# Where the modulation dot products of a two-layer decoder trunk run, and how many steps lie between a unit's scores and its transposes

## The chip, the cores and the metric

The kernel runs on one core of a Trainium2 chip. The metric is the device time of one execution in microseconds (us), as the median of the runs shown. One execution was also taken with the hardware profiler. Its times are counted from its first instruction, and its span ends with its last.

TensorE (PE) multiplies matrices and transposes. VectorE (DVE) and ScalarE (ACT) do the elementwise work and empty PSUM, the memory that TensorE writes to. SyncE (SP) issues the loads of weights. POOL issues some others.

## The reference

Two layers run over 512 positions of width 1024. Each layer is

```python
mod = c_act @ w_ada + b_ada                      # six vectors of 1024: sh1 sc1 g1 sh2 sc2 g2
h = rmsnorm(x) * (1 + sc1) + sh1
u = h @ w_in                                     # pool, conv, q, k, v, three gates
merged = sum of sigmoid(gate_i) * (mixer_i(u) @ p_i)   # pooling, short convolution, attention
x = x + g1 * (merged @ w_out)
h2 = rmsnorm(x) * (1 + sc2) + sh2
x = x + g2 * ((silu(h2 @ w_gate) * (h2 @ w_up)) @ w_down)
```

The attention has 8 heads of 64, causal, in blocks of 256: a query sees its own block, and the past block where the gate allows it. The six vectors `mod` depend on `c` alone, so they may be computed at any time before their use: `g1` is first used after the output projection, `sc2` and `sh2` at the second norm.

## The kernel before

**Matmuls.** All large products are made three times with split operands (`mm3`, high times high, high times low, low times high, L149), so a weight tile of 128x1024 is loaded into a `raw` buffer (3 of them), split into `whi` by ACT (L325) and `wlo` by DVE (L328), and used by PE for eight triples. PE's instructions stand in program order. So do the instructions that the code pins on ACT and DVE, the splits and the dot products among them; the others are placed by a scheduler.

**Order of the work in a layer.** First comes the loop along k, eight steps that make q and three feature tiles; in layer 1 it begins with halves of three steps, and after the first of them `second` norms the rest. Three more feature tiles follow, then the k stage and the v stage (two calls of `wide`, four weight tiles each), two feature tiles for the convolution, 16 gate tiles with the pool and convolution products (`p1`, `p2` per step of eight, L909 to L929), and the list `GATE2`: eight more gate tiles, with the attention products put between. `drain()` stands before the first attention product and runs whatever attention work is left. The output projection and the feed-forward part follow.

**Ticks.** `mm3` counts columns. Every 2,048 columns, that is four triples of 512, it calls `tick()`. A tick first moves the attention on and then spends credit on queued small work.

**Attention as fibers.** `attention` is a generator that goes through four pairs of heads. For each it makes q and k features by transposes (`to_features`), then starts four units, one for each 128 queries. A unit makes its scores and the softmax (L594 to L619), then waits `WAIT[i]` ticks, transposes the probabilities (`tp`, L155) into PSUM tiles from which ACT and DVE copy them (L630, L631), waits two ticks, and multiplies with v (`po`). A unit with i of 2 or 3 needs two PSUM tiles for its transposes. A pair takes 12 ticks: q features at tick 3, k features at 4, units at 6, 8, 11 and 14, the next pair's q features at 15. At one tick the attention generator acts first, and then the units in the order of their start.

**PSUM.** The tag `mm` has four tiles. Gate tiles, `p1`, `p2`, features, transposes and `po` share them. Scores have a tag of their own, `pair`, with two tiles.

**Queued work.** `bulk` is a queue of small tasks with costs. Each tick adds `bulk_rate` to the credit, which is kept to at most 4.0, and tasks run while it is not negative. `flush_bulk()` runs all that is left. `ada_tasks` makes eight dot products for one of the six vectors, each with a cost of 1.2, and an end task of 0.2. A dot product (`ada_dot`, L374) is a DVE instruction over a tile of 128x1024 that SP has loaded. With `early` the tile is one of the three `raw` buffers that the weights use; without, one of the six `w4` buffers, of which four hold q and k from the end of the loop along k until the attention has used them.

Before the change, layer 0 runs `g1`, `sc2` and `sh2`, 24 dots, in `raw` buffers during the attention (rate 0.5). Layer 1 runs `g1` in the k and v stage in `w4` buffers, four dots before each of the two `wide` calls, and `sc2` and `sh2`, 16 dots, in the attention (rate 0.35).

Of the kernel before, what the change touches and what calls it, by code (L numbers as in the profile page):

```python
# [57 lines left out]
SH1, SC1, G1, SH2, SC2, G2 = range(6)  # L58
# [19 lines left out]
def hybrid_trunk(ctx, tc, xT, ws, ada, cols, pool_w, qk_w, crow, pos, con, out):  # L78
# [40 lines left out]
    bulk = deque()  # L119
    bulk_rate, credit = [0.0], [0.0]  # L120
# [36 lines left out]
    def mm3(o, lhs, rhs, start, stop, main=True, **more):  # L157
        matmul(o, lhs[0], rhs[0], start=start, stop=False, **more)
        matmul(o, lhs[0], rhs[1], start=False, stop=False, **more)
        matmul(o, lhs[1], rhs[0], start=False, stop=stop, **more)  # L160
        if main:
            clock[0] += o.shape[-1]
            if clock[0] >= TICK:
                clock[0] -= TICK
                tick()

    def cut(pair, *ix):
        return pair[0][ix], pair[1][ix]
# [163 lines left out]
    def load_w():  # L332
        while at[1] < min(at[0] + 1 + SUMS_AHEAD, len(items)):
            sums, sub = items[at[1]]
            if sums is not None and sub == 0:
                sums.begin()
            at[1] += 1
        sums, what = items[at[0]]
        at[0] += 1
        if sums is not None:  # L340
            return sums.load(what)
        l, blocks = what
        raw = rawt()
        fetch(raw, l, blocks)
        return split_w(raw, len(blocks))
# [3 lines left out]
    def next_w(ahead=None):  # L349
        ahead = ahead_now[0] if ahead is None else ahead  # L350
        while at[0] < len(items) and len(loaded) <= ahead:
            loaded.append(load_w())
        return loaded.popleft()

    def wblk(w, b):
        return w[0][:, b, :], w[1][:, b, :]

    def wrow(w, b0):
        return (w[0][:, b0:b0 + 4, :].rearrange("p b n -> p (b n)"),
                w[1][:, b0:b0 + 4, :].rearrange("p b n -> p (b n)"))  # L360
# [16 lines left out]
    def ada_first_load(j):  # L377
        tiles = {}
        for part in (SC1, SH1):
            tiles[part] = w4([P, D])  # L380
            nc.sync.dma_start(tiles[part], ada[0, part, j])
        return tiles
# [4 lines left out]
    def ada_first(j, tiles, part):  # L387
        pin(ada_dot(tiles[part], 0, part, j))
        m = mod[0][:, part, j:j + 1]
        if part == SC1:  # L390
            A.activation(amod[0][0][:, j:j + 1], m, AF.Identity, scale=colt[:, 0, C_N1 + j:C_N1 + j + 1],
                         bias=abias[:, j:j + 1])
        else:
            A.activation(m, m, AF.Identity, bias=colt[:, 0, C_ADA + part * KT + j:C_ADA + part * KT + j + 1])

    def ada_step(l, part, j, early):
        aw = wp.tile([P, D], F32, tag="raw", name=nm("raw"), bufs=RAW) if early else w4([P, D])
        nc.sync.dma_start(aw, ada[l, part, j])
        pin(ada_dot(aw, l, part, j))

    def ada_end(l, part):
        m = mod[l][:, part]
        V.tensor_add(m, m, colt[:, l, C_ADA + part * KT:C_ADA + (part + 1) * KT])
        if part in (SC1, SC2):
            fold_scale(l, 0 if part == SC1 else 1, 0, KT)
        if part == G1:
            V.tensor_scalar(m, m, 0.5, None, op0=ALU.mult)

    def ada_tasks(l, parts, early=False):
        out = []  # L410
        for part in parts:
            for j in range(KT):
                out.append((1.2, lambda part=part, j=j: ada_step(l, part, j, early)))
            out.append((0.2, lambda part=part: ada_end(l, part)))
        return out
# [101 lines left out]
    def second(nrm, l, i, bank):  # L517

        hold[0] = None
        nrm.stat(BLOCK, S, bank)  # L520
        for k, lo, hi in HALVES[3:] + REST:
            nrm.apply(l, i, k, lo, hi)
# [48 lines left out]


    GAP = (2, 3, 3, 3)
    WAIT = (2, 3, 3, 3)

    def unit(hp, i, q, k, v, y, nrq, prq):

# [40 lines left out]
        for a in range(2):  # L618
            V.tensor_scalar(pr[a][:, :w], pr[a][:, :w], den[:, a:a + 1], None, op0=ALU.mult)  # L619
        yield WAIT[i]  # L620

# [93 lines left out]
    for l in range(L):  # L715
# [7 lines left out]
        for n, (k, lo, hi) in enumerate([(k, 0, S) for k in range(KT)] if l == 0 else HALVES + REST):  # L723
            if l == 0:
                if k + 3 < KT:
                    first.append(ada_first_load(k + 3))
                if k + 2 < KT:
                    ada_first(k + 2, first[k + 2], SC1)
                    ada_first(k + 2, first[k + 2], SH1)
                    norm.first_scaled(k + 2)  # L730
                    norm.first_hi(k + 2)
                loaded.append(load_w())
                if k + 2 < KT:
                    norm.first_lo(k + 2)
            if k not in held:
                held[k] = next_w(0 if l == 0 else None)
            if l > 0 and n == 1:
                second(norm, l, 0, bank)
            w = held[k]
            h = norm.k(k)  # L740
            for t in range(lo // P, hi // P):
                mm3(q_ps[t], cut(h, slice(None), slice(t * P, (t + 1) * P)), wrow(w, 0), k == 0, k == KT - 1)
            for z in range(3):
                mm3(f_ps[z][:, lo:hi], wblk(w, 4 + z), cut(h, slice(None), slice(lo, hi)),
                    k == 0 and lo == 0, k == KT - 1)
# [100 lines left out]
            if j == 1:  # L846
                bulk.append((0, lambda: pool_chain(1, pool1)))

        gains = ada_tasks(l, (G1,)) if l > 0 else []
        bulk.extend(gains[:4])  # L850
        k_ps = wide()
        for t in range(TT):
# [45 lines left out]
        V.tensor_mul(cv[1], pb, cv[1])  # L898
        y_conv.append(split_from(cv[1]))

        bulk.extend(ada_tasks(l, (G1, SC2, SH2)[l:], True))
        bulk_rate[0] = (0.5, 0.35)[l]
        ahead_now[0] = 3

        def gate():
# [342 lines left out]
```

## Time and profile before

| what | value |
|---|---|
| median of 3 runs | 1481.39 us (1480.77 to 1481.45) |
| the profiled execution's own time | 1480.46 us |
| its span | 1478.7 us |
| PE, DVE, ACT busy | 1456.7, 1052.2, 666.3 us |
| mean granted TensorE clock | 0.999 |

The profiled execution is 0.93 us under the median, and 1.8 us of it lie around the span. A row of the groups or of the timeline gives a line of the code, an engine, what is written from what, and durations; a bracket at its end is the idle time of that engine just before and what ended it. A row of stretches gives the busy time of each engine between two times, the granted clock and the load of the DMA engines.

### The profile page before, as it was taken

The numbers are of one execution on the slowest core, as the hardware profiler recorded it, in microseconds if no ns is written. First come the engines' busy times: TensorE is split into PE (matmuls) and PEld (weight loads), VectorE is DVE, ScalarE is ACT, GpSimd is POOL, SyncE is SP. The second block draws the span as 40 slices with busy tenths as digits, with TensorE's granted clock in tenths as the row PEclk, the third lists the DMA queues.
The fourth block names the chain that finished last, engine by engine and source line by source line (L and its number), as shares of the span: only waits on it lengthen the run. The fifth ranks groups of instructions, "written<-read, shape, count | busy, mean of one in ns | idle before, by whom it ended". The sixth has DMA issues, their size and how long they took to land.

```text
span 1478.7 us, 21940 instructions
## 1 busy us (share of the span) xinstructions
PE 1456.7 (99%) x8443; PEld 1268.0 (86%) x8443; DVE 1052.2 (71%) x1855; ACT 666.3 (45%) x1138; POOL 105.8 (7%) x157
## 2 busy tenths in 40 slices
PE   8999999999999999999999999999999999999999
PEld 6888787778988998989988877778889889989997
DVE  7976887758686876767666777776586757657672
ACT  4634555443453352535444345455335525434350
POOL 0000000001100211210000000000010102111200
PEclk9999999999999999999999999999999999999999
DMA  9514433365337775744334443333462436637431
GB/s 346 199 73 159 141 136 134 115 227 148 109 114 221 207 190 174 198 113 117 114 109 146 155 143 126 102 114 128 143 193 81 141 114 167 191 89 196 131 105 65
DMA packets 84409, 217.19 MB, mean 147 GB/s; under 512 B 10832, under 2 KB 23760, under 8 KB 84304
## 3 DMA queue, kind: packets, MB, share of 16 engines
q1 hardware_dynamic: 67456, 177.37, 35.2%
q0 software_dynamic: 16128, 37.76, 11.6%
q8 instruction: 66, 1.08, 0.3%
q10 hardware_dynamic: 720, 0.66, 0.1%
q14 instruction: 39, 0.32, 0.1%
HBM read 213.65 MB, written 2.10 MB: 146 GB/s over the span
## 4 chain that ended last, share of the span: by engine, by line
PE 84%; DVE 8%; DMA 3%; ACT 3%; issue 1%; SPq 0%; DVEq 0%; ACTq 0%
PE mm L149 72%; PE pair L149 11%; DMA raw<-in_ws 2%; DVE wlo L328 2%; PE mm L155 1%; ACT whi L325 1%; DMA w<-in_ada 1%; DVE w L374 1%; DVE raw L374 1%; ACT tmp L612 0%; DMA x<-in_xT 0%; ACT tmp L614 0%; DVE big L914 0%; SPq L232 0%; DVE big L929 0%
## 5 line engine op out<-in xcount | busy, mean ns | idle before, releaser
L149 PE MATMUL mm<-big,whi 128*128 128x512 f32 (+1 forms) x4362 | 1083.3, 340 | 5.6 <-DVE tmp L1081 2.5
L149 PEld LDWEIGHTS mm<-big,whi 128*128 128x128 f32 x4362 | 746.0, 190 | 93.6 <-DVE tmp L1081 4.1
L149 PE MATMUL mm<-big,wlo 128*128 128x512 f32 (+1 forms) x2181 | 736.1, 337 | 0.0
L149 PEld LDWEIGHTS mm<-big,wlo 128*128 128x128 f32 x2181 | 413.9, 190 | 44.7
L325 ACT ACTIVATE whi<-raw 128x1024 fp32r<-128x1024 f32 (+2 forms) x240 | 248.8, 1039 | 298.3 <-PE mm L149 231.1
L328 DVE TENSOR_TENSOR wlo<-raw,whi 128x1024 fp32r<-128x1024 f32 (+2 forms) x240 | 284.7, 1193 | 81.9 <-ACT whi L325 81.0
L325 ACT ACTIVATE whi<-w 128x1024 fp32r<-128x1024 f32 x72 | 76.2, 1059 | 147.8 <-PE mm L149 107.7
L954 DVE SCALAR_TENSOR_TENSOR x<-mm,mod,x 128x512 f32<-128x512 f32 (+1 forms) x90 | 62.0, 689 | 101.4 <-PE mm L149 101.3
L254 POOL DMA_DIRECT2D w<-in_ws x72 | 48.5, 683 | 982.1 <-DVE w L374 377.3
L328 DVE TENSOR_TENSOR wlo<-w,whi 128x1024 fp32r<-128x1024 f32 x72 | 86.7, 1220 | 31.0 <-ACT whi L325 30.2
L149 PE MATMUL pair<-whi,big 128*128 128x512 f32 x224 | 76.7, 390 | 0.0
L256 POOL DMA_DIRECT2D w<-in_ws x72 | 64.6, 923 | 153.1 <-DMA w<-in_ws 136.3
L149 PE MATMUL pair<-big,whi 128*128 128x256 f32 (+1 forms) x376 | 74.0, 294 | 0.0
L374 DVE SCALAR_TENSOR_TENSOR w<-w,csil 128x1024 f32<-128x1024 f32 x56 | 66.9, 1220 | 9.5 <-DMA w<-in_ada 9.3
L149 PEld LDWEIGHTS pair<-big,whi 128*128 128x128 f32 x376 | 60.4, 191 | 2.2
L149 PE MATMUL mm<-whi,big 128*128 128x512 f32 x160 | 57.2, 394 | 1.7 <-ACT big L497 1.4
L149 PE MATMUL pair<-big,wlo 128*128 128x256 f32 (+1 forms) x188 | 55.3, 294 | 0.0
L511 DVE TENSOR_TENSOR big<-tmp,big 128x512 fp32r<-128x512 f32 x48 | 33.0, 690 | 24.3 <-ACT big L510 23.4
L149 PEld LDWEIGHTS pair<-whi,big 128*128 128x128 f32 x224 | 42.1, 188 | 8.7
L374 DVE SCALAR_TENSOR_TENSOR raw<-raw,csil 128x1024 f32<-128x1024 f32 x40 | 48.4, 1218 | 1.2 <-DMA raw<-in_ada 1.2
L914 DVE SCALAR_TENSOR_TENSOR big<-big,mm 128x512 f32<-128x512 f32 x48 | 32.6, 682 | 21.5 <-PE mm L149 21.1
L149 PE MATMUL pair<-wlo,big 128*128 128x512 f32 x112 | 43.6, 390 | 0.0
(187 smaller groups left out, 1251.5 us busy)
## 6 DMA issues: line engine op xcount, KB each, us to landing
raw<-in_ws SPq DMA_DIRECT2D x146, 512.0 KB, 3.4
w<-in_ws POOLq DMA_DIRECT2D x144, 256.0 KB, 4.6
w<-in_ada SPq DMA_DIRECT2D x56, 512.0 KB, 5.3
raw<-in_ada SPq DMA_DIRECT2D x40, 512.0 KB, 3.2
raw<-in_ws SPq DMA_DIRECT2D x64, 256.0 KB, 4.2
raw<-in_ws SPq DMA_DIRECT2D x24, 384.0 KB, 3.5
raw<-in_ws SPq DMA_DIRECT2D x16, 448.0 KB, 5.3
raw<-in_ws SPq DMA_DIRECT2D x36, 128.0 KB, 3.0
```

Source lines behind the costliest of these rows:

```text
L149: tc.keep_in_program_order(T.matmul(*a, **k))
L155: tc.keep_in_program_order(T.transpose(*a))
L254: nc.gpsimd.dma_start(dst, self.source(0, 1))
L256: nc.gpsimd.dma_start(dst, self.source(*other), accum_op=ALU.add)
L325: A.activation(hi[:, :n], raw[:, :n], AF.Copy)
L328: ins = V.tensor_sub(lo[:, :n], raw[:, :n], f32(hi)[:, :n])
L374: return V.scalar_tensor_tensor(aw, aw, 1.0, csil, op0=ALU.mult, op1=ALU.mult, accum_out=mod[l][:, part, j:j + 1])
L511: V.tensor_sub(lo, src, f32(hi))
L914: V.scalar_tensor_tensor(sg, sg, 1.0, branch, op0=ALU.add, op1=ALU.mult)
L954: V.scalar_tensor_tensor(x[k][:, lo:hi], src, mod[l][:, part, k:k + 1], x[k][:, lo:hi], op0=ALU.mult, op1=ALU.add)
```

## The change

`WAIT` goes from three to four ticks for units 2 and 3. The eight dots of `g1` of layer 0 go from the attention to the k and v stage, as in layer 1. The eight dots of `sc2` of layer 1 go from the attention into the loop along k, after `second`, in `w4` buffers. What is left in the attention is 16 dots in layer 0 (rate 0.35) and 8 in layer 1 (rate 0.18).

```diff
-    WAIT = (2, 3, 3, 3)
+    WAIT = (2, 3, 4, 4)
...
             if l > 0 and n == 1:
                 second(norm, l, 0, bank)
+                bulk.extend(ada_tasks(l, (SC2,)))
+                bulk_rate[0] = 0.6
...
-        gains = ada_tasks(l, (G1,)) if l > 0 else []
+        gains = ada_tasks(l, (G1,))
         bulk.extend(gains[:4])
...
-        bulk.extend(ada_tasks(l, (G1, SC2, SH2)[l:], True))
-        bulk_rate[0] = (0.5, 0.35)[l]
+        bulk.extend(ada_tasks(l, (SC2, SH2)[l:], True))
+        bulk_rate[0] = (0.35, 0.18)[l]
```

## Prediction

> **What bounds the kernel now.** I read the page first, then PE's waits, then stretches of the stages that the change touches, and last the timeline round the single waits.
>
> ```profile
> span 1478.7 us, 21940 instructions
> PE 1456.7 (99%) x8443; PEld 1268.0 (86%) x8443; DVE 1052.2 (71%) x1855; ACT 666.3 (45%) x1138; POOL 105.8 (7%) x157
> PE 84%; DVE 8%; DMA 3%; ACT 3%; issue 1%; SPq 0%; DVEq 0%; ACTq 0%
> ```
>
> PE is busy in all but 22.0 us of the span, and the change removes no matmul. So nothing can be won but waits of PE. These are the ones that matter here, in order of size (engine, line, what it waited for: us, times, longest):
>
> ```profile
> PE mm L155 <- DVE tmp L619: 4.7, 5, 1.9
> PE mm L149 <- DVE tmp L1081: 2.5, 8, 0.6
> PE mm L149 <- ACT big L909: 2.4, 1, 2.4
> PE mm L149 <- DVE big L914: 1.2, 1, 1.2
> PE mm L149 <- DVE big L890: 1.1, 1, 1.1
> PE mm L155 <- DVE big L514: 0.3, 1, 0.3
> ```
>
> The row with L1081 is the feed-forward part and stays. The others, 9.7 us, lie between the v stage and the output projection of the two layers. The stretches: k and v stage of layer 0 and of layer 1, attention of layer 0 and of layer 1, the second half of layer 1's loop along k, and 4 us after one wait.
>
> ```profile
> core 0: us, PE busy (x) PEld busy (x) DVE busy (x) ACT busy (x) POOL busy (x), PEclk, DMA share, GB/s
> 74.40:127.00 52.60, 52.60 (x235) 43.59 (x235) 37.56 (x91) 21.04 (x34) 0.00 (x0) 1.00 0.25 91
> 802.00:854.60 52.60, 51.48 (x229) 42.26 (x228) 43.22 (x92) 19.34 (x31) 0.00 (x0) 1.00 0.41 141
> 127.00:305.00 178.00, 173.95 (x907) 138.97 (x907) 140.91 (x333) 88.70 (x201) 0.00 (x0) 1.00 0.41 142
> 855.00:1034.00 179.00, 174.48 (x907) 140.11 (x905) 134.50 (x321) 89.79 (x203) 0.00 (x0) 0.99 0.37 126
> 763.00:784.00 21.00, 21.00 (x95) 17.38 (x94) 6.40 (x6) 6.17 (x8) 0.20 (x1) 1.00 0.37 126
> 943.00:945.00 2.00, 1.88 (x8) 1.79 (x9) 2.00 (x3) 0.78 (x3) 0.00 (x0) 0.50 0.00 0
> 945.00:947.00 2.00, 2.00 (x8) 1.58 (x7) 2.00 (x5) 0.24 (x1) 0.00 (x0) 0.69 0.44 162
> ```
>
> In the attention DVE is busy 79% (layer 0) and 75% (layer 1), and PE waits some 4 us in each. In the loop along k DVE is busy 30%. In layer 0's k and v stage it is busy 71% and PE never waits; in layer 1, with eight dots more, 82%, and PE waits once.
>
> **The dots.** One costs 1.22 us of DVE, in either buffer:
>
> ```profile
> L374 DVE SCALAR_TENSOR_TENSOR w<-w,csil 128x1024 f32<-128x1024 f32 x56 | 66.9, 1220 | 9.5 <-DMA w<-in_ada 9.3
> L374 DVE SCALAR_TENSOR_TENSOR raw<-raw,csil 128x1024 f32<-128x1024 f32 x40 | 48.4, 1218 | 1.2 <-DMA raw<-in_ada 1.2
> ```
>
> Eight are 9.8 us. Out of layer 0's attention, DVE falls there from 140.9 to 131.1 us (74%); out of layer 1's, from 134.5 to 124.7 us (70%). None of this is PE's time; what it is worth is the waits that it feeds.
>
> *One wait behind a late weight.* In layer 1:
>
> ```profile
> 921.78 0.33 SPq L398 DMA_DIRECT2D raw<-in_ada  x1
> 924.55 10.15 SPq L232 DMA_DIRECT2D raw<-in_ws  x2
> 933.08 1.23 DVE L328 TENSOR_TENSOR wlo<-raw,whi 128x1024 fp32r<-128x1024 f32 x1
> 938.75 1.06 ACT L325 ACTIVATE whi<-raw 128x1024 fp32r<-128x1024 f32 x1 [3.77 <-DMA raw<-in_ws]
> 943.12 1.65 PE L149 MATMUL mm<-w,big 128*128 128x256 f32 x6 [2.36 <-ACT big L909]
> 943.89 1.22 DVE L374 SCALAR_TENSOR_TENSOR raw<-raw,csil 128x1024 f32<-128x1024 f32 x1
> ```
>
> A dot's tile was loaded at 921.78 and used at 943.89: one of three `raw` buffers was held for 22 us. The second weight load of 924.55 had to wait until the split at 933.08 freed another, ACT stood 3.77 us for it, the exponentials and the gate's tanh (L909) queued behind, and PE's `po` stood 2.36 us for the PSUM tile that the tanh frees. Then the granted clock was 0.50 for 2 us and 0.69 for 2 us, 1.6 us of work. So this event costs 2.4 + 1.6 = 4.0 us. The Trainium skill ("TensorE: Matmul & The Clock Gate", Why this matters for your kernels) says that the clock falls back for idle gaps above about 3 us; by it the event would have cost 2.4 us and the sum below would be 1.6 us smaller. The trace shows the fall after 2.36 us, and I go by the trace. With half as many dots in layer 1 a dot's tile stands in the way half as often: **-4.0**. Layer 0 gets the number of dots and the rate that layer 1 had, so such an event may come there: between 0 and 4.0, taken at a quarter since 16 dots made one in one layer and 24 none in the other: **+1.0**.
>
> *Backlog of DVE in layer 0.* The waits for L914 and L514 (1.2 + 0.3 us), both for PSUM tiles that DVE empties late, go with 9.8 us less work: **-1.5**, between -1.5 and 0.
>
> *The k and v stage of layer 0.* It gets what layer 1 has. There the multiplication that frees the tile for the last convolution product came late:
>
> ```profile
> 123.39 0.69 DVE L890 TENSOR_TENSOR big<-mm,big 128x512 f32<-128x512 f32 x1 [0.85 <-PE mm L149]
> 853.29 0.68 DVE L890 TENSOR_TENSOR big<-mm,big 128x512 f32<-128x512 f32 x1
> 854.12 0.70 PE L149 MATMUL mm<-big,whi 128*128 128x512 f32 x2 [1.11 <-DVE big L890]
> ```
>
> In layer 0 DVE stood idle for PE before it, in layer 1 it was behind, and PE waited 1.11 us. Layer 0 would come to 37.56 + 9.8 = 47.3 us of 52.6, 4 us above layer 1's 43.2 (the rotary tables' work among it). So 1.11 us, up to 1.1 + 4 if all of the difference came late; most of it lies ahead of idle time, so **+1.6**, between 0 and 5.
>
> *The loop along k of layer 1.* DVE has 14.6 us idle in the 21 us shown, in gaps such as this one:
>
> ```profile
> 772.40 1.22 DVE L328 TENSOR_TENSOR wlo<-raw,whi 128x1024 fp32r<-128x1024 f32 x1 [3.53 <-ACT whi L325]
> ...
> w<-in_ada SPq DMA_DIRECT2D x56, 512.0 KB, 5.3
> ```
>
> The queue is empty when the dots come, so the saved credit of 4.0 issues four at the first tick and one every other tick after. A burst of 4.9 us delays the norms of the later k-steps by as much. On SP the seventh load waits for the first dot's `w4` buffer, and weights queue behind, but they are fetched three tiles ahead. The eight loads of 512 KB, 4.2 MB, fit beside a DMA share of 0.37. I take **0**, between 0 and 1.1 (the L890 row, if one norm comes late). If that cover were gone, all eight dots, 9.8 us, would be PE's.
>
> **The fourth step.** A tick is four triples, 12 matmuls, and 12 take:
>
> ```profile
> 36.93 2.72 PE mm L149 x12
> ```
>
> So transposes of units 2 and 3 come at least 2.7 us later. The longest of the five waits for L619 (the normalised probabilities) is 1.9 us, so all should end: **-4.7**, between -4.7 and 0. Two things come in their place.
>
> First, unit 2's transposes move from unit 3's start to the tick of the next pair's q features. Then q features and two transposes, three of the four `mm` tiles, are taken at once beside the running gate. Three places per layer (the last pair has no next), six in all. The same place now:
>
> ```profile
> 162.15 0.87 PE L155 MATMUL mm<-ident,tmp 128*128 128x128 f32 x6
> 165.30 0.55 DVE L631 TENSOR_TENSOR w<-mm,w 128x384 fp32r<-128x384 f32 x1
> 165.60 0.60 PE L155 MATMUL mm<-ident,w 128*128 128x128 f32 x4
> 165.83 1.22 DVE L374 SCALAR_TENSOR_TENSOR raw<-raw,csil 128x1024 f32<-128x1024 f32 x1
> 167.05 0.68 DVE L914 SCALAR_TENSOR_TENSOR big<-big,mm 128x512 f32<-128x512 f32 x1
> ```
>
> The q features start at 165.60, so the third tile would be wanted near 166.4, and the product `p2` left its tile only at 167.73: 1.3 us late. But a dot (1.22 us) and the copy of unit 2's transposes stood ahead of it on DVE, and the copy moves behind. A place costs between 0 and 2.4 us (the L909 row); I take 0.25, nearest to the places that do not wait at all: **+1.5** for six.
>
> Second, the last unit's `po` comes one tick nearer to the attention product that needs it:
>
> ```profile
> 310.34 1.11 PE L149 MATMUL mm<-w,big 128*128 128x256 f32 x8
> 315.39 0.29 DVE L649 TENSOR_TENSOR big<-tmp,big 128x128 fp32r<-128x128 f32 x1 [0.38 <-ACT big L648]
> 318.32 0.69 DVE L914 SCALAR_TENSOR_TENSOR big<-big,mm 128x512 f32<-128x512 f32 x1 [2.64 <-PE mm L149]
> ```
>
> From the end of `po` (311.3) to that of L649 (315.7) are 4.4 us. The first attention product ended near 318.2, and its last triple, which needs the result, began 0.7 us earlier, at 317.5: 1.8 us to spare, less 2.7 us is 0.9 us short in layer 0. Part of the 4.4 us was ACT behind a late weight, so **+0.4**, between 0 and 0.9.
>
> **The sum**: -4.0 + 1.0 - 1.5 + 1.6 + 0 - 4.7 + 1.5 + 0.4 = -5.7 us. From 1480.46, the profiled execution's own time, that is 1474.8; the median of the runs is 0.93 us above that execution, so 1475.7. With every gain and no cost it is -10.2 us, 1471.2.
>
> **Rivals.**
> *The waits move and the gain is given back.* DVE is still busy 70 to 74% in the attention, the first tick there still issues four dots at once from saved credit, and a PE that no longer waits reaches the next late tile sooner. If half of the 10.2 us returns and layer 0's k and v stage and the PSUM places cost 1.6 + 1.5 + 0.4, it is -1.6 us: 1479.8. For it: waits on L914, L514 and L909 exist already. Against: the loads leave the stages where they are. That the dots do not run where they are queued comes out here too, since credit only decides the tick.
>
> *PSUM tiles (slower).* The three transposes-worth of tiles at one tick do wait, at all six places. Without that term the sum is -7.2 us, so from 1.2 us a place the change loses; at 2.0 us, between the L914 and the L909 rows, it is +4.8 us: 1486.2. For it: the 1.3 us above. Against: with that copy and some dots gone, DVE empties `p2` earlier. The Trainium skill ("Perfetto Trace Analysis", Optimization Strategy) says that a gap repeating on the engine that should be saturated can mean too few PSUM tiles; no row here shows six such gaps.
>
> *DVE over its measure in layer 0's k and v stage.* At 47.3 of 52.6 us a late rotary table or pool step pushes the chain that ends in L890. At the bound of +5 the sum is -2.3 us, 1479.1; it needs late attention on top to lose.
>
> **How the numbers follow.** Forecast 0.60, waits given back or the k and v stage at its bound 0.22, PSUM tiles 0.16, still more gain 0.02. A measurement of this kernel can tell about 0.2%, 3.0 us, from no change. Forecast and more gain are faster (0.62), the second group is within it (0.21, with a little of it beyond), the third slower (0.17). The forecast's own range is 1471.2 to 1478.4; with the others, leaving out the worst of the PSUM case, 1471 to 1485.
>
> **What would show it.** Right: no PE wait for L619; none for L909 in layer 1's attention, and the clock at 1.00 there; a wait for L890 of 1 to 2 us in both layers; PE without waits in layer 1's loop along k. Wrong: waits of L155 or L149 at q features for L914, L631 or L909; a PE wait before the first attention product over 0.9 us; a wait for L328 or L484 in layer 1's loop.

## The result and the profile after

The kernel got slower: 1487.17 us (1486.28 to 1487.35, five runs) against 1480.77 us (1477.67 to 1481.45, five runs) for the kernel before. The ratio is 1.0048, interval 1.0034 to 1.0063. The forecast was 1475.7 us with a range from 1471 to 1485, so the sign was wrong. The time is near that of the rival "PSUM tiles (slower)", 1486.2 us, which had a chance of 0.16; how far that is luck is said below.

Lines of the helpers keep their numbers up to L738. The tanh of a gate tile was L909 and is L911, the products behind it were L914 and are L916, L890 is L892, and L1081 is L1083.

The head of the page after, with the busy times:

```profile
span 1485.4 us, 21924 instructions
PE 1462.2 (98%) x8443; PEld 1273.5 (86%) x8443; DVE 1057.4 (71%) x1855; ACT 664.8 (45%) x1138; POOL 105.8 (7%) x157
```

The span grew by 6.7 us. PE's busy time grew by 5.5 us of that, with the same 8443 matmuls, so most of the growth is not idle time: 4.7 us of it is work that ran at a lower clock (the ledger below has 6.3 us of that after, and the prediction 1.6 us before). Its idle time went from 22.0 to 23.2 us. PE's waits after:

```profile
PE mm L149 <- ACT big L911: 8.6, 3, 4.0
PE mm L155 <- DVE big L514: 2.8, 1, 2.8
...
PE mm L149 <- DVE big L892: 1.0, 1, 1.0
```

The five waits for L619 and the one for L914 are gone. The tanh, with one wait of 2.4 us before, has 8.6 us in three, and L514 has one of 2.8 us. The stretches that the forecast named, in the same order (k and v stage of layer 0, attention of layer 0, second half of layer 1's loop along k), and then 4 us behind the wait for L514 and 6 to 7 us behind each of the two long waits for L911:

```profile
core 0: us, PE busy (x) PEld busy (x) DVE busy (x) ACT busy (x) POOL busy (x), PEclk, DMA share, GB/s
74.40:127.00 52.60, 52.45 (x233) 42.96 (x232) 44.62 (x106) 19.45 (x32) 0.00 (x0) 1.00 0.43 141
127.00:305.00 178.00, 175.19 (x906) 140.99 (x905) 137.30 (x320) 89.97 (x204) 0.00 (x0) 0.99 0.36 123
763.00:784.00 21.00, 21.00 (x94) 17.42 (x93) 15.56 (x24) 7.01 (x10) 0.31 (x1) 1.00 0.55 184
215.00:217.00 2.00, 2.00 (x9) 1.61 (x8) 1.46 (x4) 0.69 (x1) 0.00 (x0) 0.59 0.88 264
217.00:219.00 2.00, 2.00 (x7) 1.56 (x6) 1.09 (x1) 0.98 (x2) 0.00 (x0) 0.56 0.20 80
940.00:941.00 1.00, 0.97 (x2) 0.83 (x3) 1.00 (x4) 0.00 (x0) 0.00 (x0) 0.50 0.00 0
941.00:943.00 2.00, 2.00 (x6) 1.57 (x5) 1.19 (x2) 0.00 (x0) 0.00 (x0) 0.50 0.00 0
943.00:945.00 2.00, 2.00 (x6) 1.52 (x6) 0.00 (x0) 0.00 (x0) 0.00 (x0) 0.50 0.74 262
945.00:947.00 2.00, 2.00 (x11) 1.64 (x10) 0.08 (x1) 0.69 (x1) 0.00 (x0) 0.80 0.00 0
989.00:991.00 2.00, 1.97 (x7) 1.60 (x8) 2.00 (x4) 0.00 (x0) 0.00 (x0) 0.80 0.00 0
991.00:993.00 2.00, 2.00 (x7) 1.51 (x6) 0.79 (x2) 0.00 (x0) 0.00 (x0) 0.50 0.35 115
993.00:995.00 2.00, 2.00 (x11) 1.62 (x10) 1.29 (x2) 0.69 (x1) 0.00 (x0) 0.85 0.41 156
```

The dots in layer 1's loop along k cost nothing: seven of the eight lie in this stretch, DVE went from 6.40 to 15.56 us and PE stayed at 21.00 of 21. With eight more in layer 0's k and v stage, DVE went from 37.56 to 44.62 us and PE from 52.60 to 52.45. In layer 0's attention the dots fell from 28.01 to 19.48 us, but DVE's busy time in the stretch stayed where it was, 140.99 us after 140.91: other work filled it. The last eight rows show a clock of 0.50 to 0.85 behind each long wait.

**Where the waits stand.** At the tick of a next pair's q features, four transposes for these and six of unit 2 now run in one row. The timeline of PE at the three places that waited long:

```profile
207.95 0.60 PE L155 MATMUL mm<-ident,w 128*128 128x128 f32 x4
208.38 0.82 PE L155 MATMUL mm<-ident,tmp 128*128 128x128 f32 x6
...
214.79 0.66 PE L155 MATMUL mm<-ident,w 128*128 128x128 f32 x4 [2.81 <-DVE big L514]
...
934.80 0.60 PE L155 MATMUL mm<-ident,w 128*128 128x128 f32 x4
935.24 0.82 PE L155 MATMUL mm<-ident,tmp 128*128 128x128 f32 x6
940.03 1.22 PE L149 MATMUL mm<-big,whi 128*128 128x512 f32 x2 [3.97 <-ACT big L911]
...
983.94 0.60 PE L155 MATMUL mm<-ident,w 128*128 128x128 f32 x4
984.38 0.82 PE L155 MATMUL mm<-ident,tmp 128*128 128x128 f32 x6
989.03 0.72 PE L149 MATMUL mm<-big,whi 128*128 128x512 f32 x2 [3.83 <-ACT big L911]
```

At both places in layer 1 the row of ten transposes stands right behind the last triple of a gate tile. They take three of the four `mm` tiles, the finished gate product holds the fourth, and the next gate tile can't begin until the tanh has emptied it. What ACT does meanwhile at the second place:

```profile
934.77 1.06 ACT L325 ACTIVATE whi<-raw 128x1024 fp32r<-128x1024 f32 x1 [2.34 <-PE mm L149]
935.86 0.56 ACT L612 ACTIVATE tmp<-pair,asm,nrq 128x256 f32<-128x256 f32 x1
...
937.50 0.56 ACT L614 ACTIVATE tmp<-pair,asm,nrq 128x256 f32<-128x256 f32 x1
...
938.04 0.69 ACT L513 ACTIVATE big<-mm,colt 128x512 fp32r<-128x512 f32 x1
938.61 0.88 ACT L630 ACTIVATE w<-mm 128x384 fp32r<-128x384 f32 x2
939.35 0.63 ACT L911 ACTIVATE big<-mm 128x512 f32<-128x512 f32 x1
```

The gate's last product is complete near 935.0. The tanh starts at 939.35, behind a weight's split, four exponentials of a unit's softmax, the q features' copy and the two copies of unit 2's transposes. ACT is busy all the time; PE stands still for 3.97 us.

In layer 0 the ticks fall two triples into a gate tile, so PE has gate work left at this point, and the next to want a tile are the k features. There DVE was behind:

```profile
211.71 1.22 DVE L374 SCALAR_TENSOR_TENSOR raw<-raw,csil 128x1024 f32<-128x1024 f32 x1
...
212.85 1.22 DVE L328 TENSOR_TENSOR wlo<-raw,whi 128x1024 fp32r<-128x1024 f32 x1
213.99 0.75 DVE L514 SCALAR_TENSOR_TENSOR big<-mm,colt,big 128x512 fp32r<-128x512 f32 x1
```

A dot and a split, 2.4 us, stand ahead of the L514 that frees the q features' tile.

**The ledger.** With what the clock lost behind them (two microseconds at 0.59 lose 2 x 0.41), the three events cost 2.81 + 1.7, 3.97 + 2.9 and 3.83 + 1.7 us, 16.9 in all; a third wait for L911 is 0.8 us. Gone are 4.7 us for L619, 2.4 + 1.6 for the old event at L909, 1.2 for L914 and 0.3 for the old L514, 10.2 in all. 17.7 less 10.2 is 7.5 us, against 6.7 us of span. PE's waits elsewhere in the kernel are 1.8 us shorter after than before, so about 1 us of the growth is in none of these items.

### The profile page after: what moved, and what is told of

It is laid out like the page before. It is cut to its first block, busy times and chain, and to the rows that moved or that the text cites. A ratio compares the mean times of both kernels' runs of the same rounds, so it can differ in the third digit from the quotient of the medians.

```text
span 1485.4 us, 21924 instructions
## 1 busy us (share of the span) xinstructions
PE 1462.2 (98%) x8443; PEld 1273.5 (86%) x8443; DVE 1057.4 (71%) x1855; ACT 664.8 (45%) x1138; POOL 105.8 (7%) x157
## 4 chain that ended last, share of the span: by engine, by line
PE 87%; DVE 6%; ACT 3%; DMA 3%; issue 1%; SPq 0%; DVEq 0%; ACTq 0%
PE mm L149 75%; PE pair L149 11%; DMA raw<-in_ws 2%; DVE wlo L328 2%; PE mm L155 1%; ACT whi L325 1%; DMA w<-in_ada 1%; DVE w L374 0%; DVE raw L374 0%; DMA x<-in_xT 0%; SPq L232 0%; ACT tmp L614 0%; ACT tmp L612 0%; DVE tmp L1083 0%; DVE tmp L481 0%
## 5 line engine op out<-in xcount | busy, mean ns | idle before, releaser
L374 DVE SCALAR_TENSOR_TENSOR w<-w,csil 128x1024 f32<-128x1024 f32 x72 | 86.3, 1224 | 10.1 <-DMA w<-in_ada 9.9
L916 DVE SCALAR_TENSOR_TENSOR big<-big,mm 128x512 f32<-128x512 f32 x48 | 32.7, 686 | 25.9 <-PE mm L149 25.5
L510 ACT ACTIVATE big<-tmp 128x512 fp32r<-128x512 f32 x48 | 29.5, 620 | 20.7 <-DVE tmp L808 11.0
```

What stands on the lines that cost most here:

```text
L374: return V.scalar_tensor_tensor(aw, aw, 1.0, csil, op0=ALU.mult, op1=ALU.mult, accum_out=mod[l][:, part, j:j + 1])
L510: A.activation(hi, src, AF.Copy)
L916: V.scalar_tensor_tensor(sg, sg, 1.0, branch, op0=ALU.add, op1=ALU.mult)
```

## The experiments

The theory: the loss is the fourth step's alone, by the tiles that unit 2's transposes take at the tick of the next q features, with evacuations queued behind other work. One rival is that the moved dots cost more than they bring; another that the step is bad by what it does to unit 3 or to `po`. Ratios are to the kernel before, run beside it on the same chip, in five rounds each. The experiments ran on three chips, and the kernel before does not take the same time on each, so from chip to chip only ratios are compared.

**The dots alone.** The kernel after, with

```diff
-    WAIT = (2, 3, 4, 4)
+    WAIT = (2, 3, 3, 3)
```

> The dots are moved as in the change, the fourth step is left out (WAIT 2, 3, 3, 3). PSUM theory (the changed kernel loses some 17 us at three of the six places where unit 2's transposes and the next pair's q features take three of the four mm tiles at one tick): the ten transposes in a row are gone and with them these waits; some of the waits for L619 return, at most 4.7 us; 1471 to 1477 us. Rival, the dots (the loads and DVE work put into the k and v stage and the loop along k push attention work late): the time stays at 1483 us or more.

Measured: 1471.66 us against 1482.95, ratio 0.9928 (0.9913 to 0.9943). PE's waits of this kernel that lie in the changed stages:

```profile
PE mm L149 <- ACT big L911: 0.5, 1, 0.5
...
PE mm L155 <- DVE tmp L619: 0.3, 1, 0.3
```

The moved dots bring about 0.7%. The wait for L619 is down to 0.3 us, in a kernel whose fourth step is undone: moving the dots cured the five waits of before. In the profiled executions the time fell by 1480.46 - 1471.5 = 9.0 us and PE's idle time by 8.5 us, from 22.0 to 13.5. Most of that are the waits named here: 4.4 at L619, 2.4 - 0.5 at the tanh, 1.0 + 0.3 at L914 (now L916, 0.2 left) and L514, 0.2 at L892 (0.9 left), less a new 0.5 at L616, in sum 7.3. The 1.6 us of clock behind the old event at L909 are gone too, but this execution lost 1.7 us of clock behind a wait of 1.80 us near its start.

**The fourth step alone.** The kernel before, with

```diff
-    WAIT = (2, 3, 3, 3)
+    WAIT = (2, 3, 4, 4)
```

> The kernel before with the fourth step alone (WAIT 2, 3, 4, 4), all dots where they were. PSUM theory: the waits for L619 go (5 us), the waits at the six places come, with more dots in the way of the copies than in the changed kernel; 1483 to 1492 us. Rival, the dots: the step alone only gains, 1474 to 1478 us.

Measured: 1484.64 us against 1482.95, ratio 1.0013 (1.0002 to 1.0024). PE's waits of this kernel:

```profile
PE mm L149 <- ACT big L909: 4.6, 2, 3.8
PE mm L149 <- DVE big L914: 2.5, 2, 1.6
...
PE mm L149 <- DVE big L514: 1.9, 1, 1.9
...
PE mm L155 <- DVE big L514: 1.7, 1, 1.7
```

The waits for L619 are traded for waits on PSUM tiles, with little net. On top of the moved dots the same step costs far more, 1.0048 against 0.9928. By the spans it is 15.7 us there and 5.4 us here. Of the 10.3 us between them, 4.4 are that it has almost no wait for L619 left to remove, and 3.3 that the clock fell behind more of the new waits; the rest is in the waits themselves.

**Which unit's step.** The kernel after, with `WAIT` of unit 3 alone raised,

```diff
-    WAIT = (2, 3, 4, 4)
+    WAIT = (2, 3, 3, 4)
```

> The changed kernel with the fourth step for unit 3 alone (WAIT 2, 3, 3, 4), so that unit 2's transposes keep their tick with unit 3's scores and no tick takes three mm tiles. PSUM theory: the waits at the six places go, those for L619 come back for unit 2 only, 1 to 2 us; 1469 to 1475 us. Rival, the dots: 1483 us or more.

and with that of unit 2 alone:

```diff
-    WAIT = (2, 3, 4, 4)
+    WAIT = (2, 3, 4, 3)
```

> The changed kernel with the fourth step for unit 2 alone (WAIT 2, 3, 4, 3). PSUM theory: the ten transposes in a row and the waits behind them are all there; 1483 to 1489 us. Rival (it takes both steps together to fill the tiles): 1471 to 1476 us.

Measured: 1471.14 us, ratio 0.9922 (0.9907 to 0.9937), for unit 3, and 1488.18 us, ratio 1.0064 (1.005 to 1.0078), for unit 2. PE's waits with unit 2's step alone:

```profile
PE mm L149 <- ACT big L911: 8.6, 4, 4.0
PE mm L155 <- DVE big L514: 4.5, 2, 2.8
```

Unit 2's step is the whole loss. Unit 3's can't be told from nothing: 0.9922 against 0.9928 without it. With unit 3's alone no wait for L619 came back, where 1 to 2 us were expected; two short ones for L911, 1.4 us in sum, are left.

**Room elsewhere for unit 2's transposes.** If the `mm` tiles are what is short, transposes that take another place should not wait. In the first try they went to the two halves of a tile with the tag of the scores:

```diff
+        two = ps_pair() if i == 2 else None
...
-            tp = ps_mm().rearrange("p (j a q) -> p j a q", a=n, q=P)[:, :i + 1]
+            room = ps_mm() if two is None else two[:, aa[0]]
+            tp = room.rearrange("p (j a q) -> p j a q", a=n, q=P)[:, :i + 1]
```

> The changed kernel, but unit 2's transposes go into one pair tile (two banks) in place of two mm tiles; the step and the dots stay. PSUM theory: the ten transposes still run in a row, PE no longer waits for L911 or L514 behind them, the waits for L619 stay away; 1468 to 1473 us. Rival, the order on ACT (the gate's tanh stands behind eight exponentials and three copies, whatever tiles there are): PE still waits at these places, 1480 us or more. Rival, the dots: 1483 us or more.

Measured: 1522.45 us, ratio 1.0265 (1.0247 to 1.0282). PE's waits of this kernel:

```profile
PE pair L155 <- DVE w L633: 36.0, 8, 6.4
...
PE mm L149 <- ACT big L913: 0.8, 1, 0.8
```

This missed for a reason of its own. The loop copies the first set before it writes the second; in two tiles these overlap, but in one tile the second set waited for the copies of the first, eight times, 36.0 us. The wait for the tanh did fall, from 8.6 to 0.8 us. The second try writes both sets first and then copies both:

```diff
+        tps = []
+        for aa in groups:
+            room = ps_mm() if two is None else two[:, aa[0]]
...
+            tps.append(tp)
+        for aa, tp in zip(groups, tps):
```

> The changed kernel with unit 2's transposes in one pair tile, as in the run before that, but both sets of transposes are issued before the first copy, so that the second set does not wait for the copies of the first (that wait was 36.0 us in eight places). PSUM theory: neither that wait nor those behind ten transposes in a row (13 to 17 us in the changed kernel) are left; 1468 to 1474 us. Rival, the order on ACT (the tanh late behind exponentials and copies, whatever tiles there are): PE still waits for L911, 1480 us or more.

Measured: 1472.5 us against 1478.94, ratio 0.9955 (0.9942 to 0.9967). The place in layer 1, from the timelines of PE and ACT (the tanh is L916 here, the copy L635):

```profile
931.79 0.60 PE L155 MATMUL mm<-ident,w 128*128 128x128 f32 x4
932.22 0.82 PE L155 MATMUL pair<-ident,tmp 128*128 128x128 f32 x6
...
932.84 0.56 ACT L612 ACTIVATE tmp<-pair,asm,nrq 128x256 f32<-128x256 f32 x1
...
935.03 0.70 ACT L513 ACTIVATE big<-mm,colt 128x512 fp32r<-128x512 f32 x1
935.60 0.50 ACT L635 ACTIVATE w<-pair 128x384 fp32r<-128x384 f32 x1
935.97 0.62 ACT L916 ACTIVATE big<-mm 128x512 f32<-128x512 f32 x1
```

The same ten transposes stand in a row and the tanh is about as late behind the same exponentials, but two `mm` tiles are free and PE has no long wait here. So neither the ten transposes nor ACT's load does it alone: the tiles must be short as well. One new wait came, 1.64 us in layer 0, where `po` waits for the second copy of unit 2's transposes (L636), which DVE does behind a split.

**Where the tick falls in a gate tile.** The kernel after, with layer 1's ticks shifted by two triples, so that they fall inside a gate tile as in layer 0:

```diff
+        if l == 1:
+            clock[0] -= 2 * S
         m01, y_attn = [], []
```

> The changed kernel with the ticks of layer 1's attention two triples later, so that they fall into a gate tile, as in layer 0, and not on its end, where the next gate tile needs a PSUM tile at once. If it is the tick's place within the gate tile that makes the late tanh a wait of PE: layer 1's two long waits for L911 go or shrink below 1.5 us each, those of layer 0 stay; 1474 to 1480 us. Rival (any place does, once three tiles are taken at one tick): 1484 us or more.

Measured: 1473.86 us, ratio 0.9963 (0.9951 to 0.9976). The waits for L911 are gone. What is left is L514, 4.5 us in two, one in layer 0 as in the kernel after and a new one of 1.67 us in layer 1, which is a little more than expected. So in layer 1 the long waits come from transposes that stand right behind the end of a gate tile. Layer 0's event is there as before; that its cause is DVE is read from the timeline, as no run takes the dot and the split from its way. In this execution the clock did not fall behind it, so part of the difference to the kernel after is clock.

**Each move of dots by itself.** The kernel before, with layer 0's `g1` moved,

```diff
-        gains = ada_tasks(l, (G1,)) if l > 0 else []
+        gains = ada_tasks(l, (G1,))
...
-        bulk.extend(ada_tasks(l, (G1, SC2, SH2)[l:], True))
-        bulk_rate[0] = (0.5, 0.35)[l]
+        bulk.extend(ada_tasks(l, (SC2, SH2), True))
+        bulk_rate[0] = 0.35
```

> The kernel before with the dots of g1 of layer 0 alone moved into its k and v stage (16 left in its attention, rate 0.35); layer 1 and WAIT as before. By the traces, layer 0 gains the 4 to 5 us that its attention waits and pays up to 1.6 us in the v stage, and layer 1 keeps its waits: 3 to 5 us faster than the kernel before, the rest of the 11 us of both moves is layer 1's. Rival: layer 0's part pays it all back in the k and v stage and the 11 us are layer 1's alone; no difference.

and with layer 1's `sc2` moved:

```diff
+                bulk.extend(ada_tasks(l, (SC2,)))
+                bulk_rate[0] = 0.6
...
-        bulk.extend(ada_tasks(l, (G1, SC2, SH2)[l:], True))
-        bulk_rate[0] = (0.5, 0.35)[l]
+        bulk.extend(ada_tasks(l, (G1, SC2, SH2) if l == 0 else (SH2,), True))
+        bulk_rate[0] = (0.5, 0.18)[l]
```

> The kernel before with the dots of sc2 of layer 1 alone moved into its loop along k (8 left in its attention, rate 0.18); layer 0 and WAIT as before. If the two moves add up, this is what both gave (0.72%) less what layer 0's gave (0.33%): some 0.4%, 5 to 7 us faster than the kernel before on the same chip, with no wait of PE in the loop along k, and the long wait for L909 and those for L619 in layer 1 gone or under 1.2 us together. Rival (the moves do not add up, the step in the loop costs something): within 2 us of the kernel before.

Measured: 1473.81 us, ratio 0.9967 (0.9954 to 0.9979), for layer 0, and 1478.56 us against 1479.7, ratio 0.9995 (0.9986 to 1.0004), for layer 1. PE's waits with layer 0's move:

```profile
PE mm L149 <- ACT big L909: 2.8, 1, 2.8
...
PE mm L155 <- DVE tmp L619: 1.9, 2, 1.2
```

and with layer 1's:

```profile
PE mm L155 <- DVE tmp L619: 3.0, 4, 2.0
...
PE mm L149 <- DVE big L916: 1.2, 1, 1.2
```

In the profiles each move takes away the waits of its own layer: in the first kernel the event of layer 1 at the tanh stays, in the second the waits of layer 0 stay and the 2.4 us of that event are gone. PE's idle time falls by 4.9 and 2.7 us, and by 8.5 with both. The profiled executions are 6.0 and 4.0 us shorter than 1480.46, and 9.0 with both; in the first two that has the 1.6 us of clock in it that the profiled execution of the kernel before lost and these did not.

The medians do not agree with that. Layer 1's move came out at 0.05% where 0.4% was expected, which is the rival's "within 2 us". Its eleven runs spread from 1476.32 to 1480.7 us with a mean clock between 1.0 and 0.997, and its profile is one of the fastest two. So a gain in time is shown for layer 0's move and for both together, but not for layer 1's alone, and whether the two add up stays open.

**The better version.** The kernel after with unit 3's step alone and the shifted ticks:

```diff
-    WAIT = (2, 3, 4, 4)
+    WAIT = (2, 3, 3, 4)
...
+        if l == 1:
+            clock[0] -= 2 * S
```

> The changed kernel with the fourth step for unit 3 alone and the ticks of layer 1's attention two triples later. If the ticks' place at the end of a gate tile makes what waits for L911 are left in layer 1 (1.4 us), it is 1 to 2 us faster than with the step for unit 3 alone, a ratio of 0.990 to 0.992 to the kernel before. Rival (those waits have other causes): no difference from the step for unit 3 alone, 0.992 to 0.994.

Measured: 1467.39 us against 1479.7, ratio 0.9917 (0.9903 to 0.993). The waits for L911, L892 and L616 are gone too, but the ratio can't be told from the 0.9922 without the shift, so the shift is not shown to add anything here. The version beats both kernels.

## Why the prediction was wrong

**The step that failed: the six places, "+1.5 for six".** They cost 16.9 us in three of them and next to nothing in the others, 2.8 us a place against the 0.25 chosen. Three things went wrong in the working. The forecast looked at one place, the first of layer 0, which does not wait in the kernel after either, and took it for six. It asked when the third tile at that tick comes free of `p2`; where PE did wait, it was for the next user of a tile after the transposes. In layer 0 that is the k features, and the tile is freed by L514 behind a dot and a split. In layer 1 the ticks stand otherwise against the gate tiles, so it is the next gate tile, and the tile is freed by a tanh on ACT, whose queue was not read. And the upper bound, 2.4 us from the row of the old event, was taken without the 1.6 us of clock that the same event had been charged with a few paragraphs earlier.

The rival named the mechanism ("do wait, at all six places"). It was at three, at 4.5 to 6.9 us each where it had 2.0, so 16.9 us in place of 12. That its time came within 1 us is luck: the rest of the change brought some 11 us (17.7 us of new waits and clock less the 6.7 us of span) where its sum had 7.2.

**A gain put to the wrong part: "-4.7" for the fourth step.** The five waits for L619 went with the dots alone (0.3 us left), and they also went with the step alone. The forecast let the dots take away only L914, L514 and the event at L909. The sum of the whole change is not altered by that, since the waits did go. But on top of the dots the step had at most some 0.3 us to bring, so by the forecast's own costs it was worth -0.3 + 1.5 + 0.4 = +1.6 us, a loss, and could have been left out.

**The dots were right, and under-sized.** By the forecast's terms they make -4.0 + 1.0 - 1.5 + 1.6 + 0 = -2.9 us; the profiled execution of the dots alone gives -9.0. Most of the difference is the 4.4 us at L619, and the two costs that did not come: the event of a late weight in layer 0 (+1.0; none there with 16 dots) and the k and v stage of layer 0 (+1.6), where PE lost 0.15 us as the stretch shows. The -4.0 for the event in layer 1 was taken whole, though the reason given for it, half as often, makes it -2.0; in the kernel with the dots alone the event is gone. The wait for L892 stayed at 1.0 in layer 1 and did not come to layer 0, so "1 to 2 us in both layers" was wrong in a small thing. And DVE's busy time in layer 0's attention, which was to fall to 131.1 us, stayed at 140.99 in the same stretch, while the waits for L619 and L914 there went. So the share of busy time did not show what the move was worth. Whether it was the dots' place in DVE's queue or their loads that made these waits is not separated by a run.

**Right.** No wait for L619 in the kernel after; PE without a wait in layer 1's loop along k, at 0 as forecast; no wait before the first attention product, where +0.4 was charged. "The clock at 1.00" in layer 1's attention was wrong, by the new events. The rival of DVE over its measure in the k and v stage did not happen. The sentence of the Trainium skill that the rival drew on ("Perfetto Trace Analysis", Optimization Strategy), that a repeating gap can mean too few PSUM tiles, is borne out here, though at three of six places: with two tiles elsewhere the gap of 3.97 us went.

## What to carry to other kernels

When a change makes several things want PSUM tiles at one point of the program, list for that point who holds each tile and read, on the engine that empties it, everything queued ahead of the instruction that does: the price is that queue (4.4 us here), not the length of the copy. Do it for each place that differs in what comes next, since the same step cost next to nothing at three places and 4.5 to 6.9 us at three others. And when either of two parts of a change would end the same wait, price each part on top of the other: the second is worth only what the first leaves, and here that was less than its cost.

## What the hardware showed that was not expected

The clock fell behind waits shorter than expected, but not behind every wait of such a length. It was 0.50 to 0.59 behind idle times of PE of 2.36 us (before), 2.81, 3.83 and 3.97 us (after). It also fell near the start of the kernel with the dots alone, behind 1.80 us, to 0.61 from 19 to 21 us and 0.53 from 21 to 23. It did not fall behind 2.80 us in the kernel with layer 0's dots moved:

```profile
938.22 0.98 PE L149 MATMUL mm<-w,big 128*128 128x256 f32 x6 [2.80 <-ACT big L909]
...
939.00:941.00 2.00, 2.00 (x11) 1.67 (x10) 2.00 (x4) 0.38 (x1) 0.00 (x0) 1.00 0.00 0
```

nor behind 2.82 us in the kernel with shifted ticks, at the very place where the kernel after lost 1.7 us behind 2.81 us:

```profile
214.36 0.66 PE L155 MATMUL mm<-ident,w 128*128 128x128 f32 x4 [2.82 <-DVE big L514]
...
215.00:217.00 2.00, 2.00 (x11) 1.62 (x10) 1.46 (x3) 1.24 (x2) 0.00 (x0) 1.00 0.75 248
```

So the length of a wait alone does not decide it, and what does stays open. Where the clock fell, it stood at one half for about 3.4 us, or twice that: two microseconds at 0.59 and two at 0.56 have lost 1.7 us, which is 3.4 us at one half. A wait of 2.4 to 2.8 us therefore cost 1.6 to 1.7 us more in some executions and nothing more in others. That is also the size of the spread between runs of one kernel: for layer 1's dots alone, a mean clock of 0.997 in place of 1.0 is 4.4 us over the span, and the runs spread over 4.4 us. The Trainium skill ("TensorE: Matmul & The Clock Gate", Why this matters for your kernels) says to keep such gaps under about 3 us; here the falls behind 2.36 and 2.81 us show that this is not enough.
